# Handing out an attention unit in three parts per iteration in place of two, at higher shares

## The chip, the cores and the metric

The kernel runs on one core of a Trainium2 chip. The metric is the device time of one execution in microseconds (us); lower is better. Given are the times of three runs of the kernel before the change, and one execution with the hardware profiler on.

## The reference

Two blocks follow each other on 512 tokens of width 2048. The first is a pooling mixer with modulation by a conditioning vector, ended by a normalisation. The second block projects its normalised input with one wide matrix and runs three attentions on the result; the change touches these three alone:

```python
# A: sliding window, 12 heads of 64, 4 key heads, window 128, a sink per head
scores = einsum('bnqkgd,bnskd->bnkgqs', qb, kb) * (d ** -0.5)
p = exp(scores + bias - m); denom = sum(p) + exp(sink - m)
# B: forgetting attention, 12 heads of 64, causal, decay cq - ck added to the scores
# C: 4 heads of 128 over 256 memory tokens
ya = attention(...); ua = (ya * silu(za)) @ w_branch_a      # B and C alike
y = g0 * ua + g1 * ub + g2 * uc;  return x + y @ w_out
```

Queries and keys are RMS-normalised per head before the scores.

## The kernel before, in words

All weights stream from HBM in 512 KB tiles issued on SyncE's queue (`Stream._dma`, line 59). Each is split into two halves; of each half ScalarE writes a rounded part `whi` (line 91) and VectorE the rest `wlo` (line 92), and every product is three matmuls: high by high, high by low, low by high (`mm3`, line 260; the matmul itself is line 258). Halves are split two ahead of their use (`take`, line 116), into four buffers. These products are called the dense stream here.

**Steps and lanes.** A projection handles 16 halves (`tile_steps`, line 265); after every three dense matmuls it calls `step()` (line 241). `step` adds the rate of the generator at the head of a lane to the lane's credit, and for each whole unit of credit runs that generator to its next `yield` (`advance`). So a generator that was put aside with `aside(gen, rate)` (line 254) hands out one part, the code up to a `yield`, every 1/rate steps. A part's instructions go to the engines' queues at that place; each engine works its queue in program order.

**Attention.** Six units are put aside one after the other: C, then A in two units, then B in three (lines 1257 to 1263). Each runs beside the two projections of the next unit (the last beside the gate logits): 64 steps of the first, 56 of the second, then `drain()` (line 1244) runs what is left without pause. A unit is the generator `attend` (line 953). Its *prelude* is: Silu of `z` (line 960), `head_norm` in 9 parts (squares line 852, sums line 853, root line 311, products lines 862 and 867), with the split of `v` beside it (lines 949, 950), then head transposes: 5 parts in A, 6 in B, 4 in C (`transp_split` line 877, `transp_stack` line 888, copied out of PSUM on lines 879, 892, 894 by ScalarE and 880, 896 by VectorE).

Then follow *items*, a head and a stretch of its query blocks: 2 per head in A and C, 3 per head in B. A, B and C have 12, 12 and 8 items per unit. For item `e`:
- `s0(e)`: scores on TensorE (bank s0 or s1), maximum on VectorE (line 1084; in A bias and maximum, lines 1080, 1082, 1087), exponentials into `pt` on ScalarE (line 1089).
- `s2(e)`: transposes of `pt` on TensorE (line 1111, bank s2), then a rounded copy `pth` on ScalarE (line 1136) and the rest `ptl` on VectorE (line 1138).
- `s4(e)`: only for the last item of a head, the value product from `vhl` and `pth`, `ptl`, 6 to 8 matmuls into bank s3 (line 258 again); it puts the head on the list `later`.
- `release(h)` copies the product out of PSUM into `os` (lines 1029, 1030); `finish(h)` makes the divisor and the gated normaliser `un` (lines 1037 to 1043); `flush` transposes `un` one iteration later (line 1172) and multiplies (line 1173).

An iteration has two parts. The first is `release` for the heads in `later`, `s0(e)`, `flush`, `finish`. The second is `s4(e - 2)` and, behind it, `s2(e - 1)`. So `s2(e - 2)` and `s4(e - 2)` are two parts apart. `pth` and `ptl` have one buffer each, `pt` two.

Of the kernel before, what the change touches and what calls it, by code (L numbers as in the profile page):

```python
# [122 lines left out]
def build(tc, nc, x, vecs, bgate, fg, sinks, bforget, w_mod, w_pin, w_grp, w_pout, mem, w_in, w_kv,  # L123
          w_ba, w_bb, w_bc, w_out, ident, tri, dmask, rel, csel, edge, out):
    es = ExitStack()
    with es:
        _build(es, tc, nc, x, vecs, bgate, fg, sinks, bforget, w_mod, w_pin, w_grp, w_pout, mem, w_in, w_kv,
               w_ba, w_bb, w_bc, w_out, ident, tri, dmask, rel, csel, edge, out)


def _build(es, tc, nc, x, vecs, bgate, fg, sinks, bforget, w_mod, w_pin, w_grp, w_pout, mem, w_in, w_kv,
# [91 lines left out]
    def bank(tag, name=None):  # L223
        return psp.tile([P, 512], F32, tag=tag, name=name or tag)
# [25 lines left out]
    def drain(lane=0):  # L250
        while lanes[lane]:
            advance(lane)

    def aside(gen, rate=1.0, lane=0):
        lanes[lane].append((gen, rate))

    def mm(ps, lhsT, rhs, start=False, stop=False):
        PE.matmul(ps, lhsT=lhsT, rhs=rhs, start=start, stop=stop)  # L258

    def mm3(ps, sh, sl, mh, ml, start, stop):  # L260
        mm(ps, sh, mh, start=start)
        mm(ps, sh, ml)
        mm(ps, sl, mh, stop=stop)
# [568 lines left out]
    def new_qk():  # L832
        return a3.tile([P, NT, 524], F32, tag="qk", name="qk")

    def new_vz():
        return a3.tile([P, NT, 512], F32, tag="vz", name="vz")
# [116 lines left out]
    def attend(kind, unit, qk, vz):  # L953
# [65 lines left out]
        def release(h):  # L1019

            s = hs[h]
            if kind == "C":
                os_[0] = a3.tile([P, T], F32, tag="os", name="os")
                S.copy(os_[0], s["o"])
                return
            if h % 2 == 0:
                os_[0] = a3.tile([P, T], F32, tag="os", name="os")
            here, there = slice(64 * (h % 2), 64 * (h % 2) + 64), slice(64 - 64 * (h % 2), 128 - 64 * (h % 2))
            S.copy(os_[0][here, :], s["o"][there, :])
            V.tensor_tensor(out=os_[0][here, :], in0=s["o"][here, :], in1=os_[0][here, :], op=add)  # L1030

        def finish(h):

            s = hs.pop(h)
            if kind == "A":
                se = a3.tile([P, NT], F32, tag="se", name="se", bufs=2)
                S.activation(se, s["nm"], AF.Exp, bias=snk[:, h0 + h : h0 + h + 1])
                V.tensor_tensor(out=s["den"], in0=s["den"], in1=se, op=add)
            V.reciprocal(s["den"], s["den"])
            if kind == "C" or h % 2 == 0:  # L1040
                un_[0] = a3.tile([P, NT, P], F32, tag="un", name="un")
            u = un_[0] if kind == "C" else un_[0][:, :, 64 * (h % 2) : 64 * (h % 2) + 64]
            V.tensor_tensor(out=u, in0=z[:, :, h * d : (h + 1) * d], in1=s["den"].unsqueeze(2).to_broadcast([P, NT, d]), op=mult)
            if kind == "C":
                pend.append([un_[0], 12 + h, 0, os_[0]])
            elif h % 2:
                pend.append([un_[0], {"A": 3 * unit, "B": 6 + 2 * unit}[kind] + h // 2, 0, os_[0]])
# [92 lines left out]
        def s4(e):  # L1140
            h, segs = items[e]
            if segs[-1][0] != NT - 1:
                return
            s = hs[h]
            o = s["o"] = bank("s3")

            order = (0, 2, 1, 3) if kind == "A" else range(nk)
            for x, k in enumerate(order):
                q0 = first(k) * P
                ob = o[:, q0 : q0 + wide(k) * P]  # L1150
                ph, pl = s["ph"][:, off[k] : off[k + 1]], s["pl"][:, off[k] : off[k + 1]]
                st_, sp_ = x == 0, x == nk - 1
                if kind == "C":
                    mm3(ob, vv[:, k, h, :128], vv[:, k, h, 128:], ph, pl, st_, sp_)
                else:
                    v = vv[:, k, h // 3 if kind == "A" else h, :]
                    mm(ob, v, ph, start=st_)
                    mm(ob, v, pl, stop=sp_)
            later.append(h)
# [4 lines left out]
        def flush(e, force=False):  # L1164

            for q in pend:
                q[2] += 1
            if pend and (force or pend[0][2] > 0):
                un, chunk, _, os = pend.pop(0)
                b = bank(S4[(e + 1) % 2])  # L1170
                for tt in range(NT):
                    PE.transpose(b[:, tt * P : (tt + 1) * P], un[:, tt, :], idf)
                V.tensor_tensor(out=ur[chunk], in0=b, in1=os, op=mult)

        ne = len(items)
        for e in range(ne + 2):
            for h in later:
                release(h)
            if e < ne:
                s0(e)  # L1180
            flush(e)
            while later:
                finish(later.pop(0))
            yield
            if e >= 2:
                s4(e - 2)
            if 1 <= e <= ne:
                s2(e - 1)
            yield
# [20 lines left out]
    qk, vz = new_qk(), new_vz()  # L1210
# [25 lines left out]
    def proj(dst, last):  # L1236
        banks = [bank(t) for t in M4]

        def ev(tt, ps):
            scaled(tt, dst[:, tt, 0:512], ps, tt)  # L1240

        for kp in range(8):
            if last and kp == 7:
                drain()
            tok_tile(banks, 2 * kp, h_h, h_l, kp == 0, kp == 7, evac=ev)
# [6 lines left out]
    for (c0, n), ev in zip(CG[1:], (ev1, ev2)):  # L1252
        cb = [bank(t) for t in M4]
        for kp in range(8):
            tok_tile(cb, 2 * kp, h_h, h_l, kp == 0, kp == 7, n=n, evac=ev)
    drain()
    aside(attend("C", 0, qk, vz), 0.34)
    for kind, unit in (("A", 0), ("A", 1), ("B", 0), ("B", 1), ("B", 2)):
        qk2 = new_qk()
        proj(qk2, False)  # L1260
        vz2 = new_vz()
        proj(vz2, True)
        aside(attend(kind, unit, qk2, vz2), 0.41)


    p4 = ExitStack()
# [150 lines left out]
```

## Time and profile before

| what | us |
|---|---|
| runs of the kernel before | 2258.87, 2262.62, 2263.61 |
| their median | 2262.62 |
| the profiled execution: its own time | 2262.3 |
| its span, first to last instruction | 2260.5 |
| TensorE busy | 2210.4 |
| VectorE busy | 1146.5 |
| ScalarE busy | 883.5 |

The granted TensorE clock averaged 0.994 of full over the span. In the profile PE is TensorE's matmuls, DVE is VectorE, ACT is ScalarE, and L258 is line 258 of the kernel. A matmul's recorded duration is longer than the distance to the next, because matmuls overlap; distances between starts are the measure of pace. A row of a timeline has the start and the duration in us, the engine, line and operation, what is written and read, and in square brackets how long the engine sat idle before it and who released it. The attention units begin near 790 us (C), 897 and 1012 (A), 1128, 1240 and 1355 (B) and end near 1465.

### The profile page before, as it was taken

What the parts mean: (1) busy time and instruction counts of PE and PEld (TensorE: products, weight loads), DVE (VectorE), ACT (ScalarE), POOL (GpSimd) and SP (SyncE); (2) the same over time, 40 slices, a digit from 0 to 9 for tenths busy, and PEclk for the clock granted to TensorE, in tenths of its full rate; (3) what the DMA queues carried; (4) which work ended last, traced back from release to release, by engine and by line L of the source; (5) the groups of instructions that cost most, each with busy time, mean ns of one, the idle gap of its engine ahead of it and who ended that gap; (6) DMA issues with size and microseconds to landing.
All of it is one profiled execution on the core that took longest, in us unless ns stands there. A gap on an engine that the chain in (4) does not pass through costs nothing.

```text
span 2260.5 us, 26829 instructions
## 1 busy us (share of the span) xinstructions
PE 2210.4 (98%) x10199; PEld 1819.0 (80%) x10199; DVE 1146.5 (51%) x1997; ACT 883.5 (39%) x1719; POOL 0.2 (0%) x4
## 2 busy tenths in 40 slices
PE   7999999999999999999999999999999999999999
PEld 4678888888889988787778787788888888888887
DVE  3676665346665454757564645554334235326333
ACT  4433363333334354545464646442232222224221
POOL 0000000000000000000000000000000000000000
PEclk9989999999999999999999999999999999999999
DMA  9856633347674322222222222233333333333543
GB/s 334 276 164 217 202 99 98 94 122 231 225 224 120 105 75 75 75 75 75 75 75 75 75 75 75 66 98 99 94 93 103 96 100 94 102 94 98 154 131 112
DMA packets 164809, 275.12 MB, mean 122 GB/s; under 512 B 11090, under 2 KB 63048, under 8 KB 164424
## 3 DMA queue, kind: packets, MB, share of 16 engines
q1 hardware_dynamic: 164680, 273.41, 39.6%
q8 instruction: 80, 1.31, 0.2%
q14 instruction: 49, 0.40, 0.1%
HBM read 264.98 MB, written 8.39 MB: 121 GB/s over the span
## 4 chain that ended last, share of the span: by engine, by line
PE 82%; DVE 7%; ACT 5%; DMA 3%; issue 2%; SPq 0%; DVEq 0%; ACTq 0%
PE m L258 53%; PE s L258 26%; DVE wlo L92 2%; DVE qk L896 1%; DMA raw<-w_kv 1%; ACT pt L1089 1%; PE s L1111 1%; ACT whi L91 1%; DMA raw<-w_pout 1%; ACT qk L892 1%; DVE nm L1082 1%; DVE pt L1080 0%; DVE ptl L1138 0%; DVE acc L452 0%; PE colb L258 0%
## 5 line engine op out<-in xcount | busy, mean ns | idle before, releaser
L92 DVE TENSOR_TENSOR wlo<-raw,whi 128x512 fp32r<-128x512 f32 (+2 forms) x740 | 493.4, 675 | 759.6 <-ACT whi L91 744.7
L91 ACT CAST whi<-raw 128x512 fp32r<-128x512 f32 (+2 forms) x740 | 441.4, 608 | 872.5 <-PE m L258 385.4
L258 PE MATMUL m<-whi,h_h 128*128 128x512 f32 (+2 forms) x960 | 373.3, 389 | 1.7 <-ACT whi L91 1.1
L258 PE MATMUL m<-wlo,h_h 128*128 128x512 f32 (+2 forms) x960 | 363.0, 378 | 2.9 <-DVE wlo L92 2.6
L258 PE MATMUL m<-whi,h_l 128*128 128x512 f32 (+2 forms) x960 | 362.6, 378 | 0.0
L258 PE MATMUL m<-h_h,whi 128*128 128x512 f32 x768 | 304.2, 396 | 0.0
L258 PE MATMUL m<-h_h,wlo 128*128 128x512 f32 x768 | 301.4, 392 | 1.2 <-DVE wlo L92 1.2
L258 PE MATMUL m<-h_l,whi 128*128 128x512 f32 x768 | 301.1, 392 | 0.0
L258 PEld LDWEIGHTS m<-wlo,h_h 128*128 128x128 f32 x960 | 181.1, 189 | 31.9 <-DVE wlo L92 6.1
L258 PEld LDWEIGHTS m<-whi,h_l 128*128 128x128 f32 x960 | 180.7, 188 | 31.5
L258 PEld LDWEIGHTS m<-whi,h_h 128*128 128x128 f32 x960 | 181.2, 189 | 28.6 <-ACT whi L91 1.4
L258 PE MATMUL s<-h_h,whi 128*128 128x512 f32 x512 | 200.8, 392 | 0.0
L258 PE MATMUL s<-h_l,whi 128*128 128x512 f32 x512 | 200.4, 391 | 0.0
L258 PE MATMUL s<-h_h,wlo 128*128 128x512 f32 x512 | 200.4, 391 | 0.0
L258 PEld LDWEIGHTS m<-h_h,wlo 128*128 128x128 f32 x768 | 145.4, 189 | 32.6 <-DVE wlo L92 1.7
L258 PEld LDWEIGHTS m<-h_h,whi 128*128 128x128 f32 x768 | 145.6, 190 | 30.3 <-ACT whi L91 0.5
L258 PEld LDWEIGHTS m<-h_l,whi 128*128 128x128 f32 x768 | 145.5, 190 | 29.4
L258 PEld LDWEIGHTS s<-h_h,whi 128*128 128x128 f32 x512 | 97.1, 190 | 20.3
L258 PEld LDWEIGHTS s<-h_l,whi 128*128 128x128 f32 x512 | 97.0, 189 | 20.3
L258 PEld LDWEIGHTS s<-h_h,wlo 128*128 128x128 f32 x512 | 96.9, 189 | 20.3
L258 PE MATMUL m<-whi,y_h 128*128 128x512 f32 x256 | 102.6, 401 | 1.4 <-DVE t L778 1.4
L258 PE MATMUL m<-whi,y_l 128*128 128x512 f32 x256 | 99.9, 390 | 0.0
(239 smaller groups left out, 2739.6 us busy)
## 6 DMA issues: line engine op xcount, KB each, us to landing
raw<-w_mod SPq DMA_DIRECT2D x96, 512.0 KB, 4.3
raw<-w_in SPq DMA_DIRECT2D x96, 512.0 KB, 3.7
raw<-w_pin SPq DMA_DIRECT2D x58, 512.0 KB, 3.8
raw<-w_in SPq DMA_DIRECT2D x96, 256.0 KB, 3.0
raw<-w_pout SPq DMA_DIRECT2D x32, 512.0 KB, 4.4
raw<-w_out SPq DMA_DIRECT2D x32, 512.0 KB, 3.7
raw<-w_in SPq DMA_DIRECT2D x32, 384.0 KB, 3.4
raw<-w_kv SPq DMA_DIRECT2D x16, 512.0 KB, 6.6
```

The source lines that it names most:

```text
L91: self.nc.scalar.copy(h3, v)
L92: self.nc.vector.tensor_tensor(out=l3, in0=v, in1=h3.bitcast(F32), op=ALU.subtract)
L258: PE.matmul(ps, lhsT=lhsT, rhs=rhs, start=start, stop=stop)
L892: S.activation(hi[r, :], b[r, :], AF.Copy, scale=gain[r, :])
L896: V.scalar_tensor_tensor(out=outs[e][1][w, :], in0=b[r, :], scalar=gain[r, :], in1=r32(hi[r, :]), op0=mult, op1=sub)
L1082: V.tensor_reduce(out=s["nm"][:, qt : qt + m], in_=w, axis=AX.X, op=vmax)
L1089: S.activation(pt[:, c0 : c0 + n], (pt if kind == "A" else b)[:, c0 : c0 + n], AF.Exp, bias=s["nm"][:, qt : qt + 1], accum_out=s["den"][:, ...
L1111: PE.transpose(b[:, x * P : (x + 1) * P], pt[:, c : c + P], idf)
```

## The change

An iteration hands out three parts in place of two. The value product `s4(e - 2)` stands first, as a part of its own, from the third iteration on; then `release`, `s0(e)`, `flush`, `finish`; then `s2(e - 1)` alone. So `s2(e - 2)` and `s4(e - 2)` are one part apart. The share of unit C goes from 0.34 to 0.42, that of the A and B units from 0.41 to 0.51.

```diff
         for e in range(ne + 2):
+            if e >= 2:
+                s4(e - 2)
+                yield
             for h in later:
                 release(h)
             if e < ne:
...
             while later:
                 finish(later.pop(0))
             yield
-            if e >= 2:
-                s4(e - 2)
             if 1 <= e <= ne:
                 s2(e - 1)
             yield
...
-    aside(attend("C", 0, qk, vz), 0.34)
+    aside(attend("C", 0, qk, vz), 0.42)
...
-        aside(attend(kind, unit, qk2, vz2), 0.41)
+        aside(attend(kind, unit, qk2, vz2), 0.51)
```

## Rows read from the trace of the kernel before

**Rows 1.** The page: busy time, share of span and instructions, by engine.

```profile
PE 2210.4 (98%) x10199; PEld 1819.0 (80%) x10199; DVE 1146.5 (51%) x1997; ACT 883.5 (39%) x1719; POOL 0.2 (0%) x4
```

**Rows 2.** Waits of PE, 780 to 1470 us: total us, times, longest.

```profile
PE s L1172 <- DVE un L1043: 6.4, 4, 2.2
PE s L1111 <- DVE ptl L1138: 3.7, 2, 2.0
PE s L888 <- DVE qk L862: 3.4, 4, 1.1
...
PE s L258 <- DVE ptl L1138: 1.6, 2, 0.8
```

**Rows 3.** Timeline of PE, last head of the second A unit.

```profile
1104.83 0.60 PE L1111 MATMUL s<-idf,pt 128*128 128x128 f32 x4
...
1106.66 0.40 PE L258 MATMUL m<-whi,h_h 128*128 128x512 f32 x1
...
1108.04 0.28 PE L258 MATMUL s<-pth,vhl 128*128 128x256 f32 x1
...
1108.39 0.28 PE L258 MATMUL s<-ptl,vhl 128*128 128x256 f32 x1
```

**Rows 4.** Timeline of PE and DVE, first two heads of the first A unit.

```profile
936.59 0.60 PE L1111 MATMUL s<-idf,pt 128*128 128x128 f32 x4
...
939.19 0.68 DVE L1138 TENSOR_TENSOR ptl<-s,pth 128x512 fp32r<-128x512 f32 x1
...
945.43 0.60 PE L1111 MATMUL s<-idf,pt 128*128 128x128 f32 x4
...
950.35 0.68 DVE L1138 TENSOR_TENSOR ptl<-s,pth 128x512 fp32r<-128x512 f32 x1
```

**Rows 5.** Timeline of PE and DVE, two heads of B units.

```profile
1174.34 0.60 PE L1111 MATMUL s<-idf,pt 128*128 128x128 f32 x4
...
1177.60 0.42 DVE L1138 TENSOR_TENSOR ptl<-s,pth 128x256 fp32r<-128x256 f32 x1 [0.44 <-ACT pth L1136]
...
1438.30 0.60 PE L1111 MATMUL s<-idf,pt 128*128 128x128 f32 x4
...
1440.59 0.42 DVE L1138 TENSOR_TENSOR ptl<-s,pth 128x256 fp32r<-128x256 f32 x1 [0.44 <-ACT pth L1136]
...
1442.85 0.39 PE L258 MATMUL s<-pth,vhl 128*128 128x512 f32 x1
...
1443.77 0.28 PE L258 MATMUL s<-ptl,vhl 128*128 128x256 f32 x1
```

**Rows 6.** Timeline of PE and DVE, preludes of C, A and B.

```profile
807.92 0.68 DVE L862 TENSOR_TENSOR qk<-qk,hrr 128x512 f32<-128x512 f32 x1
...
809.70 0.60 PE L877 MATMUL s<-idf,qk 128*128 128x128 f32 x4
...
924.06 0.63 PE L877 MATMUL s<-idf,mkv 128*128 128x128 f32 x4 [0.30 <-DVE qk L896]
...
1164.45 0.89 PE L1111 MATMUL s<-idf,pt 128*128 128x128 f32 x3 [1.35 <-ACT pt L1089]
```

**Rows 7.** Groups of DVE, 892 to 1008 us: count, busy us, mean ns, idle.

```profile
L92 DVE TENSOR_TENSOR wlo<-raw,whi 128x512 fp32r<-128x512 f32 x33 | 22.5, 688 | 18.2 <-ACT whi L91 18.2
```

**Rows 8.** Timeline of PE, then busy time of a stretch, its granted clock 0.61.

```profile
960.61 1.09 PE L1172 MATMUL s<-idf,un 128*128 128x128 f32 x4 [2.15 <-DVE un L1043]
961.35 0.78 PE L258 MATMUL m<-whi,h_h 128*128 128x512 f32 x1
...
964.70 0.28 PE L258 MATMUL s<-pth,vhl 128*128 128x256 f32 x1
...
960.60:964.90 4.30, 4.29 (x15) 3.65 (x16) 3.17 (x6) 1.56 (x5) 0.00 (x0) 0.61 0.31 58
```

**Rows 9.** Timeline of ACT, in the last B unit.

```profile
1406.63 1.28 ACT L1296 ACT_TABLE_LOAD   x1
1407.92 0.63 ACT L1296 ACTIVATE g<-g 128x512 f32<-128x512 f32 x1
```

## The prediction

> **What bounds the kernel now.** First the page's busy shares: TensorE is busy for 2210.4 of 2260.5 us [rows 1], so time can only come from its idle time, and any new idle time of it is time lost. Next the waits of TensorE alone, over the stretch in which attention runs beside the projections, 780 to 1470 us: the largest are the transposes of the gated normaliser `un` behind VectorE, 6.4 us in 4 waits, and score transposes behind `ptl`, 3.7 us in 2; the value product waits only twice, 1.6 us in all [rows 2]. So the value product is hidden today. Then the timelines of TensorE and VectorE around single heads, for the slack behind that hiding; there the change bites.
>
> The unit of pace is a step, three dense matmuls. Six of them, two steps, take from 1106.66 to 1108.04, so a step is 0.69 us [rows 3]. A share of 0.41 hands out a part every 2.44 steps, in twos and threes; 0.51 hands one out every 1.96 steps, practically always two; unit C goes from 2.94 to 2.38.
>
> **The change part by part.** No instruction is added or removed, and no DMA is moved against the weight stream: SyncE's queue holds only weight loads here and POOL's nothing, so that costs nothing. What moves is order and pace.
>
> *The parts fit.* Counting yields, a unit of kind A goes from 45 to 57 parts, B from 46 to 58, C from 36 to 44; divided by the shares, 110 to 112, 112 to 114 and 106 to 105 steps, of 120 before the drain. Nothing is left for the drain: cost 0.
>
> *Value product.* `s4(e-2)` came two parts after `s2(e-2)`, 4.88 steps; now it is the very next part, two steps. After a head's last transposes began at 1104.83, the dense matmul two steps on began at 1106.66 [rows 3], so the value product will now come 1.83 us after the start of the transposes. In kind A its fourth matmul needs the last `ptl`, 0.35 us later (1108.04 to 1108.39), so 2.18 in all. The first head of A had it 3.28 us after (936.59; 939.19 and 0.68), the second 5.60 us after (945.43; 950.35 and 0.68) [rows 4]. Waits of 1.10 and 3.42 us follow. The second is late because `release` and `finish` of the head before, and a projection's eviction, stood ahead on VectorE; in the new order `finish` sits with the other score part, so I take the first: 5 heads (the last of a unit has no scores ahead of it) x 2 units x 1.10 = 11.0, less the 1.6 already paid: **+9.4**, ends -1.6 (all hidden) and +20 (two heads of each unit as the second). In kind B the last `ptl` is needed 0.92 us into the product (1442.85 to 1443.77), so by 2.75. It comes at 3.68 (1174.34; 1177.60 and 0.42) or at 2.71 (1438.30; 1440.59 and 0.42) [rows 5]: waits 0.93 or none. Early heads of a unit are like the first, late ones like the second: 6 of 12, **+5.6**, ends 0 and 11. What is queued behind this wait is the dense stream itself, on TensorE.
>
> *Prelude.* The parts before the first scores (norms, head transposes) keep their number but come faster, and they were already late: a unit starts with table loads, Silu and squares on ScalarE. In A the fifth set of head transposes, 13 parts in, waits on VectorE (924.06, 0.30 idle) [rows 6]. 13 parts take 31.7 steps now and 25.5 then, 6.2 x 0.69 = 4.3 us less cover. In that time one to two weight halves less are split; a VectorE split costs 0.69 [rows 7], so 0.9 us comes back: +3.4 per unit, 2 units, **+6.8**. In B the first score transposes, 18 parts in, wait 1.35 us for the exponentials (1164.45) [rows 6], so there is no slack: 43.9 to 35.3 steps is 5.9 us less cover, two splits less give back 1.4: +4.5, 3 units, **+13.5**. In C the first transposes came at 809.70 and their last input was ready at 808.60 (807.92 and 0.68) [rows 6]: 5.1 steps are 3.5 us, less 1.1 of slack and 0.9 of splits: **+1.5**. Low end for all three, 0, if the engines had unseen room; high end, no split saved: 8.6 + 17.7 + 2.4 = 29, against 21.8 taken.
>
> *What gets easier.* An iteration, one part of each kind, lasts 5.88 steps in place of 4.88, 0.69 us more. The `un` transposes come one iteration after `finish`; each of 4 waits shrinks by that, and VectorE catches up while TensorE waits in the value product. I take 5 of the 6.4 us; ends 2.8 (pace alone) and 6.4. The first of them slowed the clock: the granted clock was 0.61 of full from 960.60 to 964.90, part of the stretch at the lower level of 1.2 GHz, and nine dense matmuls took 3.35 us (961.35 to 964.70) in place of 2.07 at 0.23 each: 1.3 us [rows 8]. Together **-6.3**. The `ptl` waits in the last unit fall by 0.69 each and a little more: **-2**, ends 0 and -3.7.
>
> *Clock.* That fall followed a wait of 2.15 us [rows 8]; the prelude waits forecast above are longer. Two new falls at 1.3: **+2.6**, ends 0 and 10 x 1.3 = 13 (two in each A and B unit).
>
> *Table loads.* In the last unit Sigmoid evictions of the gate logits alternate with exponentials. A load there took 1.28 us and the activation behind it began 0.01 later (1406.63; 1407.92) [rows 9]. The new order may add or save a pair, 2.6 us of ScalarE, mostly covered: 0, ends -2.6 and +2.6. The Trainium skill, ScalarE: Activation LUTs, "What ACT_TABLE_LOAD costs", counts a drain of about 1.4 us with each load, 2.66 together; by it the pair would be 5.3 and the ends -5.3 and +5.3. The trace disagrees, with 0.01 us in the place of the drain.
>
> *Sum.* 9.4 + 5.6 + 6.8 + 13.5 + 1.5 - 6.3 - 2 + 2.6 = +31.1. The profiled execution took 2262.3 us (span 2260.5), 0.3 below the median of the runs, 2262.62. Forecast: 2262.3 + 31.1 = 2293.4 us.
>
> **The rivals.** *Only the value product pays (slower, little):* the preludes are bound by chains that the removed cover did not hold up, and their waits stay. For it: C's prelude shows no wait today. Against it: in A and B TensorE stands at those places already, so less cover must show. Then 9.4 + 5.6 - 6.3 - 2 = +6.7, 2269. Without the gain at `un` it is 2275.
>
> *Faster:* the value product stays hidden. The place is the chain from score transposes to `ptl`: with `release` and `finish` gone from ahead of it and the load spread over longer iterations, the last `ptl` would be ready by 2.18 us (A) and 2.75 us (B) after the transposes' start. That is the deciding point. If it holds, and the preludes do not grow, `un`, `ptl` and the value product's own waits go, 6.4 + 3.7 + 1.6 with 1.3 of clock: -13, 2249. For it: B's later heads have it at 2.71. Against it: A's first head, with no `finish` ahead of it, needed 3.28 [rows 4], and the exponentials and the cast on ScalarE stay ahead of it in the same order.
>
> *No effect:* gains at `un` cancel waits at the value product and the preludes hide; within 0.2%, 2262. That the change does nothing is excluded, since the order of the parts is the program order of every engine.
>
> **How the numbers follow.** The forecast's case, both preludes and value product paying, 2280 to 2315 by its ends: 0.60. The little-slower rival, 2268 to 2280: 0.22. Faster: 0.11. No effect: 0.07. A measurement of this kernel can tell about 0.2%, 4.5 us, from no change; so faster 0.11, same 0.07, slower 0.82. The range of 2265 to 2314 takes in both slower cases and leaves out the faster one, most of no effect and the top of the high ends, in which all clock falls happen.
>
> **What would show it.** In the waits of TensorE: a group of the value product on `ptl` or `pth` of 10 to 20 us in some 15 to 20 waits (now 1.6 in 2); head transposes behind `qk` of line 862 from 3.4 us [rows 2] to 8 or more; score transposes behind the exponentials at the start of the first B unit from 1.35 us [rows 6] to over 3; `un` from 6.4 to under 3. TensorE's clock below full in stretches after 2 us waits at the beginnings of A and B units. The stretches outside 780 to 1470 us unchanged in length. The forecast is wrong if the value product's waits stay under 4 us (then the engines' chain is shorter than in the old order), or if the prelude waits do not grow (then their ends are set by something that moves with TensorE).

## The result: 1.8% slower, and the profile after

The changed kernel takes 2302.31 us (median of 4 runs, 2301.82 to 2304.67) against 2263.11 for the kernel before: ratio 1.0179, 95% interval 1.0161 to 1.0196. Its profiled execution took 2304.67 us, the longest of the four, span 2302.9, mean granted clock 0.987 (before 0.994; the other three after the change had 0.989).

First the page's busy line, which answers to [rows 1]:

```profile
PE 2240.4 (97%) x10199; PEld 1831.1 (80%) x10199; DVE 1150.6 (50%) x1997; ACT 884.8 (38%) x1719; POOL 0.2 (0%) x4
```

Same instructions, and VectorE and ScalarE as busy as before within some 4 us. TensorE is *busy* 30 us longer, though it does the same work. So a sum of idle rows won't find the whole loss. Next, one window over the attention stage in both kernels (length, then busy us and count of PE, PEld, DVE, ACT, POOL, then the granted clock, the DMA share and GB/s), before:

```profile
780.00:1510.00 730.00, 707.08 (x3486) 587.46 (x3485) 410.64 (x823) 377.93 (x810) 0.00 (x0) 1.00 0.27 77
```

and after, with 720 us of the stretch behind attention:

```profile
780.00:1510.00 730.00, 693.73 (x3319) 565.14 (x3318) 392.48 (x789) 358.47 (x775) 0.00 (x0) 0.98 0.25 72
1510.00:2230.00 720.00, 720.00 (x3176) 595.62 (x3175) 288.93 (x429) 207.65 (x342) 0.00 (x0) 1.00 0.36 104
```

Behind attention TensorE is never idle and the clock is full. In the stage its idle time grew from 22.9 to 36.3 us, and in the same time it issued fewer matmuls. The waits of TensorE after, same window, to be read against [rows 2]:

```profile
PE s L888 <- DVE qk L862: 12.8, 18, 1.1
PE s L258 <- ACT pth L1136: 8.8, 8, 2.7
PE s L1111 <- ACT pt L1089: 4.8, 3, 2.2
PE s L258 <- DVE ptl L1138: 4.5, 11, 0.5
...
PE s L877 <- DVE qk L862: 0.5, 1, 0.5
PE s L1172 <- DVE un L1043: 0.3, 2, 0.2
```

The `un` waits (6.4) and those of score transposes on `ptl` (3.7) are gone. In their place stand the value product, 13.3 us in 19 waits (`pth` and `ptl` together; it was 1.6 in 2), and the head transposes of the preludes, 12.8 in 18 (3.4 in 4). Waits of TensorE in all: 51 in the groups of the full list against 22.

**The third head of the first A unit.** The timeline of TensorE after the change:

```profile
966.10 0.60 PE L1111 MATMUL s<-idf,pt 128*128 128x128 f32 x4
...
967.92 0.28 PE L258 MATMUL s<-pth,vhl 128*128 128x256 f32 x1
...
970.08 0.38 PE L258 MATMUL s<-pth,vhl 128*128 128x256 f32 x1 [1.76 <-ACT pth L1136]
970.92 0.58 PE L258 MATMUL s<-ptl,vhl 128*128 128x256 f32 x1 [0.46 <-DVE ptl L1138]
```

The timeline of ScalarE at the same place:

```profile
967.47 0.40 ACT L1089 ACTIVATE pt<-pt,nm 128x128 f32<-128x128 f32 x1 [3.30 <-DVE nm L1087]
...
968.37 0.67 ACT L840 ACTIVATE qk<-m,r 128x512 f32<-128x512 f32 x1
968.94 0.61 ACT L91 CAST whi<-raw 128x512 fp32r<-128x512 f32 x1
969.45 0.58 ACT L1136 CAST pth<-s 128x512 fp32r<-128x512 f32 x1
```

And that of VectorE, its last `ptl`:

```profile
970.18 0.68 DVE L1138 TENSOR_TENSOR ptl<-s,pth 128x512 fp32r<-128x512 f32 x1
```

The value product arrives 1.82 us behind the transposes (966.10 to 967.92), as worked out. `pth` starts only at 969.45. In ScalarE's order three things stand ahead of it: the exponentials of the next item, which begin only at 967.47 because VectorE's maximum comes late (ScalarE sat idle for 3.30 us), then a projection's eviction (line 840) and a weight split (line 91). The last `ptl` ends at 970.86, 4.76 after the transposes. TensorE stands for 1.76 + 0.46 us.

The same exponentials also hold up heads with no eviction ahead of `pth`. For the first head of this unit the transposes start at 936.59 before [rows 4] and at 938.37 after. ScalarE's next exponentials, before and then after:

```profile
937.04 0.40 ACT L1089 ACTIVATE pt<-pt,nm 128x128 f32<-128x128 f32 x1 [2.38 <-DVE nm L1087]
```

```profile
939.76 0.40 ACT L1089 ACTIVATE pt<-pt,nm 128x128 f32<-128x128 f32 x1 [2.39 <-DVE nm L1087]
```

They begin 0.45 us behind the transposes before and 1.39 after. TensorE starts the scores that they belong to 2.54 us ahead of the transposes before (934.05) and only 1.85 after (936.52), since the parts now follow each other faster. So the last `ptl` comes 4.21 us behind the transposes (942.58) in place of 3.28, and this head waits 1.19 + 0.46 us.

**A wait without a bracket.** In TensorE's timeline after the change, the product of the first head of the first B unit shows no idle time at all:

```profile
1199.26 0.40 PE L258 MATMUL s<-pth,vhl 128*128 128x512 f32 x1
1199.50 0.49 PE L258 MATMUL s<-ptl,vhl 128*128 128x512 f32 x1
...
1200.51 0.39 PE L258 MATMUL s<-pth,vhl 128*128 128x256 f32 x1
1200.97 0.39 PE L258 MATMUL s<-ptl,vhl 128*128 128x256 f32 x1
...
1201.36 0.44 PE L258 MATMUL m<-whi,h_h 128*128 128x512 f32 x1
```

Yet it lasts from 1199.26 to the next dense matmul at 1201.36, 2.10 us; in the kernel before the same head took 1.22 (1178.88 to 1180.10). The starts lie 0.24 to 0.46 apart where 0.12 to 0.24 are usual, since the matmuls wait for a `pth` or `ptl` just written (one `pth` ends at 1200.46 and its matmul starts at 1200.51, the last `ptl` at 1200.91 and its matmul at 1200.97), and the recorded durations stretch over these gaps. Summed from first start to the start of what follows, the 28 value products take 33.67 us before and 53.35 after, and one wait of 2.69 stands ahead of a first matmul: 22.4 us more, of which the rows call only 11.7 idle.

**The prelude of the first B unit**, in TensorE's timeline after the change: head transposes, then the dense stream:

```profile
1164.94 0.30 PE L888 MATMUL s<-idf,qk 128*128 128x128 f32 x1 [0.67 <-DVE qk L862]
1166.05 0.33 PE L888 MATMUL s<-idf,qk 128*128 128x128 f32 x1 [0.81 <-DVE qk L862]
1166.65 0.33 PE L888 MATMUL s<-idf,qk 128*128 128x128 f32 x1 [0.27 <-DVE qk L862]
1167.86 0.33 PE L888 MATMUL s<-idf,qk 128*128 128x128 f32 x1 [0.88 <-DVE qk L862]
...
1168.99 0.63 PE L258 MATMUL m<-wlo,h_h 128*128 128x512 f32 x1
1169.42 0.63 PE L258 MATMUL m<-whi,h_l 128*128 128x512 f32 x1
```

Four transposes, each alone, follow VectorE's products (line 862) one by one. Then dense matmuls start 0.43 apart (1168.99 to 1169.42) in place of 0.23: the granted clock has fallen. Windows over three of the nine such stretches:

```profile
916.00:924.00 8.00, 6.21 (x24) 4.85 (x25) 5.73 (x14) 3.36 (x5) 0.00 (x0) 0.79 0.29 71
...
1040.00:1050.00 10.00, 7.07 (x22) 5.21 (x22) 7.30 (x18) 3.24 (x5) 0.00 (x0) 0.66 0.24 64
...
1165.00:1173.00 8.00, 6.04 (x22) 4.47 (x23) 5.74 (x9) 2.94 (x5) 0.00 (x0) 0.79 0.22 66
```

A mean of 0.79 over 8 us is 3.4 us at the lower level (1.2 GHz, half of full), so 1.7 us of full-speed work lost. Five stretches lie at preludes (from 919, 1042, 1168, 1288 and 1407 us; the one at 1042 is twice as long), four at value products (from 943, 970, 1097 and 1462). The nine add up to 34 us at half clock against 6.8 in two stretches before: (34 - 6.8) / 2 = 13.6 us.

### The profile page after: what moved, and what is told of

Same layout as the page of the kernel before. It is cut to its first block, busy times and chain, and to the rows that moved or that the text cites. A ratio compares the mean times of both kernels' runs of the same rounds, so it can differ in the third digit from the quotient of the medians.

```text
span 2302.9 us, 26821 instructions
## 1 busy us (share of the span) xinstructions
PE 2240.4 (97%) x10199; PEld 1831.1 (80%) x10199; DVE 1150.6 (50%) x1997; ACT 884.8 (38%) x1719; POOL 0.2 (0%) x4
## 4 chain that ended last, share of the span: by engine, by line
PE 80%; DVE 8%; ACT 6%; DMA 3%; issue 2%; SPq 0%; DVEq 0%; ACTq 0%
PE m L258 52%; PE s L258 26%; DVE wlo L92 2%; ACT whi L91 1%; ACT pt L1089 1%; DMA raw<-w_kv 1%; DVE ptl L1138 1%; DMA raw<-w_pout 1%; DVE acc L452 1%; DVE nm L1082 1%; PE s L1111 1%; DVE qk L896 1%; DVE pt L1080 1%; DVE qk L862 0%; DMA xg_d<-xg 0%
## 5 line engine op out<-in xcount | busy, mean ns | idle before, releaser
L258 PE MATMUL m<-whi,h_h 128*128 128x512 f32 (+2 forms) x960 | 378.0, 394 | 2.0 <-ACT whi L91 1.9
L258 PEld LDWEIGHTS s<-h_h,whi 128*128 128x128 f32 x512 | 97.0, 189 | 20.5 <-ACT whi L91 0.4
```

## Experiments

The prediction's theory is called "both" in the expectations: the value product and the preludes each pay, alone too. Against it stand theories by which one cause pays it all. The kernel before had a median of 2261.46 us (7 runs) beside the first four experiments and 2261.4 (20 runs) beside the others. The waits shown are TensorE's, 780 to 1510 us. A fall is a stretch below full clock in the attention stage.

**1. Only the shares, with the old two parts.**

```diff
-    aside(attend("C", 0, qk, vz), 0.34)
+    aside(attend("C", 0, qk, vz), 0.42)
...
-        aside(attend(kind, unit, qk2, vz2), 0.41)
+        aside(attend(kind, unit, qk2, vz2), 0.51)
```

> The old order of the parts, two per iteration, with the new shares 0.42 and 0.51. Theory both (order and shares each cost): the preludes are squeezed as in the changed kernel, +20 us with their clock falls, and the normaliser waits grow since an iteration is 3.9 steps: 2280 to 2290 us, head-transpose waits of 12 us or more, value-product waits small. Rival order (the value product's place is all): within 4 us of 2263. Rival shares (the shares are all): about 2302.

2308.41 us, ratio 1.0209 (1.0191 to 1.0227), 7 falls.

```profile
PE s L888 <- DVE qk L862: 13.0, 17, 1.1
PE s L1172 <- DVE un L1043: 10.3, 4, 2.7
PE s L1111 <- DVE ptl L1138: 8.8, 8, 2.6
```

Missed, 18 us above the upper end, and as slow as the change itself: taken alone, this time is nearest to what the rival "shares" foresaw (2302). The preludes wait as in the change (13.0). But two parts at 0.51 also shorten the iteration, to 2/0.51 = 3.9 steps, so the waits of the items for `un` and `ptl` grow, which stood there already [rows 2]. The experiment moved two things at once; the next ones part them by setting the unit's share anew where the items begin.

**2. The change, with preludes at the old pace** (items at 0.40 and 0.53, so an iteration of some 5.7 steps).

```diff
+        lanes[0][0] = (lanes[0][0][0], 0.40 if kind == "C" else 0.53)
         ne = len(items)
...
-    aside(attend("C", 0, qk, vz), 0.42)
+    aside(attend("C", 0, qk, vz), 0.34)
...
-        aside(attend(kind, unit, qk2, vz2), 0.51)
+        aside(attend(kind, unit, qk2, vz2), 0.41)
```

> The changed kernel with its preludes at the old shares (0.34, 0.41) and its items at 0.40 and 0.53, so that a unit still ends before the drain. Theory both: the prelude part of the loss, about 20 us with its clock falls, goes: 2280 to 2285 us, value-product waits stay at 11 to 15 us, head-transpose waits back to 5. Rival order: 2298 or more. Rival shares: 2265 or less.

2280.21 us, ratio 1.008 (1.0065 to 1.0095), 5 falls.

```profile
PE s L1111 <- ACT pt L1089: 6.4, 3, 2.2
PE s L258 <- ACT pth L1136: 5.6, 6, 1.3
PE s L258 <- DVE ptl L1138: 3.9, 10, 0.5
PE s L888 <- DVE qk L862: 2.6, 4, 0.9
```

As "both" had it: the head transposes are back at 2.6 us, 22.1 us of the loss are gone, and the value product still waits, 9.5 us in 16 waits (11 to 15 had been expected).

**3. Three parts at the new shares, in the old order:** scores, value product, transposes, so that the product again comes two parts behind its transposes.

```diff
             if e >= 2:
                 s4(e - 2)
+                yield
             if 1 <= e <= ne:
```

(on the kernel before, with the two shares of experiment 1)

> Three parts and the new shares, but in the old order: scores, value product, transposes; the value product is two parts behind its transposes. Theory both: the value product's waits (13 us) and their clock falls go, the preludes stay squeezed, the smaller normaliser waits stay: 2278 to 2286 us. Rival order: 2263 or less. Rival shares: 2298 or more.

2286.33 us, ratio 1.0112 (1.0094 to 1.0129), 8 falls.

```profile
PE s L888 <- DVE qk L862: 12.9, 18, 1.1
...
PE s L258 <- ACT pth L1136: 1.3, 1, 1.3
```

The value product's waits fall to 1.6 us (1.3 on `pth`, 0.3 on `ptl`); `un` and `ptl` of line 1111 don't come back. The largest wait that remains is the prelude's. Undoing the order alone is worth 16.0 us. Against experiment 1, from which only the third part differs, it is 22.1 us faster: at these shares the third part is needed.

**4. Only the order, with old shares and two parts:** the value product goes into the first part, ahead of the scores.

```diff
-            for h in later:
+            done = list(later)
+            for h in done:
                 release(h)
+            if e >= 2:
+                s4(e - 2)
             if e < ne:
...
-            while later:
+            for h in done:
...
-            if e >= 2:
-                s4(e - 2)
```

> The old shares and two parts per iteration, with the value product moved ahead of the scores into the first part, so one part (2.44 steps) behind its transposes. Theory both: value-product waits of 8 to 12 us with two or three clock falls, preludes as before, normaliser waits not relieved by longer iterations: 2270 to 2280 us. Rival order: 2285 or more, most of the loss. Rival shares: within 4 us of 2263.

2282.36 us, ratio 1.0097 (1.008 to 1.0114), 7 falls (counted in an execution of 2287.43 us, the longest of four). Some 2 us above the expectation.

```profile
PE s L258 <- DVE ptl L1138: 7.7, 12, 1.3
PE s L258 <- ACT pth L1136: 7.4, 8, 1.3
PE s L888 <- DVE qk L862: 3.4, 4, 1.1
```

At the old pace the product one part behind its transposes waits 15.1 us in 20 waits, with an unchanged prelude (3.4); 8 to 12 us and two or three falls had been expected. The rival "shares", which asked for 2263, falls. The `un` waits vanish here too, without a longer iteration: the value product, with its waits, now stands ahead of the `un` transposes in the same part, and `un` is ready by then.

**5. Three parts, the old order, preludes at the old pace:** experiment 3 with the share line of experiment 2. Against experiment 2 the order alone differs.

> Three parts in the old order (scores, value product, transposes), preludes at the old shares, items at 0.40 and 0.53. Theory both: neither cost is left, and the longer iteration takes away the normaliser waits (6.4 us), the ptl waits (3.7 us) and their two clock falls (1.7 us each): 2249 to 2256 us. Rival (the third part costs by itself, by cutting the dense stream more often): 2262 or more.

2256.05 us, ratio 0.9977 (0.9968 to 0.9986), 1 fall. Faster than the kernel before, by 5 us, at the upper edge of the expectation; the third part doesn't cost by itself.

```profile
PE s L1111 <- ACT pt L1089: 6.4, 3, 2.2
PE s L888 <- DVE qk L862: 2.6, 4, 0.9
PE s L1172 <- DVE un L1043: 1.7, 2, 0.8
```

**6. The same with slower preludes** (0.30 for C, 0.36 for A and B) and items at 0.42 and 0.56 to make up for it.

> The same with the preludes slower still (0.30, 0.36) and the items faster (0.42, 0.56). Theory both: the remaining prelude waits (5 us at head transposes, some of the 3 to 6 us at the first score transposes) go too, 3 to 6 us less than the run with the old prelude shares: 2245 to 2252 us. Rival (the item parts at 1.8 steps become too dense): no faster than that run.

2247.9 us, ratio 0.9946 (0.9932 to 0.996), 2 falls: it beats both kernels, the changed one by 54 us.

```profile
PE s L1111 <- ACT pt L1089: 3.9, 3, 1.5
```

The head transposes of line 888 wait no more (2.6 us in experiment 5). Both rates moved in this run, so the share of each in the gain isn't shown. In the window over the stage (columns as above) TensorE is idle for 11.0 us:

```profile
780.00:1510.00 730.00, 718.99 (x3537) 597.84 (x3536) 415.97 (x832) 383.41 (x819) 0.00 (x0) 1.00 0.27 78
```

**7. The kernel before, with only the preludes faster** (0.42 and 0.51; items back at 0.34 and 0.41).

```diff
+        lanes[0][0] = (lanes[0][0][0], 0.34 if kind == "C" else 0.41)
         ne = len(items)
```

(and the two shares of experiment 1)

> The kernel before with its preludes alone at the new shares (0.42, 0.51); items in the old order, two parts, at the old shares 0.34 and 0.41. Theory both: the prelude term by itself, head-transpose waits of about 13 us, score-transpose waits of about 5, four to six clock falls at the beginnings of units: 2277 to 2285 us beside 2262 before. Rival (the prelude waits came from what the new item order left behind): within 4 us of before.

2286.78 us, ratio 1.011 (1.0096 to 1.0124), 8 falls. A little above the expectation.

```profile
PE s L888 <- DVE qk L862: 11.7, 16, 1.1
PE s L1172 <- DVE un L1043: 7.7, 4, 3.4
PE m L258 <- DVE g L1296: 4.5, 1, 4.5
```

Prelude pace alone costs 25.4 us, in a kernel whose items keep their order and pace. Not all of it is paid in the preludes: the items come at another time within the projections, and one dense matmul beside the gate logits waits 4.5 us for VectorE. Idle time grew by only 8.6 us (22.9 to 31.5); six more falls at 1.7 us are another 10.2. Beside this run, experiment 1 says what the faster items cost in two parts: 2308.41 - 2286.78 = 21.6 us.

**8. The kernel before, with only slower preludes in A and B** (0.34, then items at 0.43; C as before).

> The kernel before, two parts in the old order, with slower preludes in A and B (0.34) and items at 0.43. Theory both: head-transpose waits from 5.0 to under 2 us, first score transposes from 3.2 to under 2, normaliser waits slightly up since an iteration is 4.65 steps: 2255 to 2260 us beside 2262. Rival: no difference, the prelude chain is not covered at any of these shares.

2255.75 us, ratio 0.9975 (0.9966 to 0.9984), 1 fall. As expected: the head transposes wait no more, and two parts per iteration keep their `un` and `ptl` waits. Two waits of dense matmuls for an eviction (line 840) are new:

```profile
PE s L1172 <- DVE un L1043: 5.1, 4, 2.2
PE m L258 <- ACT qk L840: 4.4, 2, 2.2
PE s L1111 <- DVE ptl L1138: 4.1, 5, 1.7
```

**A path from before to after**, by medians, with one main thing changed at each step (in the last the items' share also goes from 0.40 and 0.53 to 0.42 and 0.51; in the first the items' share rises together with the third part):

| step | us | difference |
|---|---|---|
| before | 2261.4 | |
| third part, old order, old prelude pace (experiment 5) | 2256.05 | -5.4 |
| value product moved to the front (experiment 2) | 2280.21 | +24.2 |
| preludes at the new pace (the change) | 2302.31 | +22.1 |

The effects don't simply add: moving the product costs 20.9 at the old pace (experiment 4) and 16.0 at the new prelude pace (experiment 3 against the change); the preludes cost 25.4 in the old kernel (experiment 7). The kernel before took 2263.11, 2261.46 and 2261.4 us beside the change, experiments 1 to 4 and experiments 5 to 8. With each time taken against its own, the steps of the path are -5.4, +24.1 and +20.5, and the 16.0 is 14.3.

## Why the prediction was right, and where it was short

The mechanism is shown: of the three things in the change, the longer iteration helps a little, and the order and the prelude pace cost some 14 to 25 us each, each in a kernel with the other one left out. The forecast of 2293.4 was 9 us short. That it came so near is in part luck: the clock and the value product were priced too low by some 18 us together, the waits of the preludes too high by 12.

- *The parts fit, nothing for the drain; nothing outside the stage:* right. TensorE isn't idle from 1510 to 2230 us, as before.
- *Value product, A: +9.4, a term that was too small.* Its arrival was right (1.82 in the row against 1.83 forecast). By lengths, starts to starts, the two A units' products grew by 13.7 us. The step that was mis-sized is "in the new order `finish` sits with the other score part, so I take the first". It takes over the first head's 3.28 us from the old pace; at the new pace the next scores come closer ahead of the transposes, their exponentials stand later ahead of `pth`, and the first head waited 1.65 (1.10 forecast; 0.97 in the second unit). The third of each unit waited 2.2, with an eviction on top. For the late second head of [rows 4] the prediction had named an eviction too, and set that head aside; it should have counted as a case that returns. One such head in each unit, at its 3.42, would have given 8 x 1.10 + 2 x 3.42 - 1.6 = 14.0.
- *Value product, B: +5.6:* 8.6 measured, 5.9 in lengths and 2.7 in the one wait ahead of a product. The first head lost 1.22 to 2.10, 0.88 (0.93 forecast), all of it in stretched starts with no idle row.
- *Preludes: +21.8, too large as waits.* The idle rows of lines 877 and 888 rose from 5.0 to 13.3 us, and the first score transposes' waits for exponentials from 3.2 to 4.8, together +9.9. The 22.1 of the path agrees only because it holds more than these waits: from experiment 2 to the change idle time grew by 10.2 us (26.1 to 36.3), 3.8 of it in the value products (9.5 to 13.3), and the falls, five in one and nine with one double in the other, took 8.5 us more. The place was partly another, too: the first B unit's score transposes were to wait over 3 us and waited 1.30 (1.35 before). The lack of cover shows earlier, in the head transposes.
- *What gets easier: -8.3 with `ptl`:* `un` fell by 6.1 and `ptl` by 3.7, more than forecast in idle time, while the third part alone gives -5.4 in time (experiment 5; there 1.7 of `un` stays and `pt` waits 3.2 us longer). Experiment 4 suggests that in the change part of it comes from the waiting in the value product and not from the pace.
- *Clock: +2.6, the term that was furthest off.* "Two new falls at 1.3" became seven, one of them double: +13.6. The prediction expected falls behind waits of 2 us, as in [rows 8]; its high end, 13 us for ten falls, is what was lost.
- *Table loads: 0.* Right in number, 8 loads for the exponentials and 3 for the Sigmoid in both kernels. But a load of 1.28 us (1458.88) stood between the maximum and the exponentials ahead of `pth` in the one product wait of 2.69.
- *The rivals:* "only the value product pays" falls with experiment 7, "faster" with experiments 2 and 4, "no effect" with the result.

The two profiled spans differ by 42.4 us. Of these, 2.7 lie ahead of the first unit, which begins at 792.7 in place of 790.0; 13.4 are idle time in the stage, 13.6 lower clock, and 10.7 starts stretched inside the value products (22.4 less the 11.7 marked idle). The kinds overlap a little, since two of the products ran partly at half clock. The 2 us that are left were not measured apart.

## What to carry to other kernels

When work is handed out by a rate, a faster rate shortens the cover of the prelude too, which here cost about as much as the reordering; give the prelude and the loop rates of their own and slow the one that is late (experiments 6 and 8). Before a consumer is moved nearer to its producer, list all that can stand ahead of the producer's copies on their engines, the next item's work, evictions and weight splits included, at the new pace and not at the old one, and price the worst head as one that returns. On the engine that bounds the kernel, compare distances between starts, and not idle rows alone: nearly half of the 22.4 us that the value products grew by stood in rows marked busy. And give the clock a term of its own for short waits: here it cost as much as the idle time did (13.6 and 13.4 us).

## What was not expected of the hardware

In the kernel before the granted clock fell after one wait of 2.15 us [rows 8]. After the change it also fell with no wait above 0.88 us near it: behind the four single transposes at 1164.94 to 1167.86, whose waits add up to 2.63 us, dense matmuls ran 0.43 apart. Over the ten profiles, kernels with 32 to 53 waits of TensorE between 780 and 1510 us had 5 to 9 falls in the stage, those with 14 to 22 had 1 or 2. The step in time between the two groups (2263.11 and less; 2280.21 and more) is wider than the step in idle time (22.9 us in the kernel before, 26.1 in experiment 2); part of the rest is lower clock, part starts stretched in the value products. What sets off a single fall isn't shown.
